# Half-height score products filled up with zeros, and the carried state of two heads in one product, in a two-block transformer layer

## The chip, the core and the metric

The kernel runs on one core of a Trainium2 chip. Its time is the device time of one execution in microseconds (us); several executions give a median. The engines named here are TensorE (matrix products, results in PSUM), VectorE, ScalarE, GpSimd and the DMA queues that SyncE issues.

## The reference, cut to what matters

Two transformer blocks run one after the other on 512 tokens of width 1024. The first block's mixer adds a chunked state-space scan and a causal attention with forget gates. The second block has a sliding-window attention, a gated spatial mixer and 32 routed experts. The parts that the change touches:

```python
# first block, state-space scan: 16 heads of 64, 4 chunks of 128 tokens, state of 128
scores = cb[:, :, None] * decay_in
y_diag = jnp.einsum('bgecls,bcsgep->bclgep', scores, xc)
...
decay_out = jnp.exp(a_cs).transpose(0, 3, 4, 1, 2)
y_off = jnp.einsum('bclgn,bcgepn->bclgep', Cc, prev_states) * decay_out[..., None]
return (y_diag + y_off).reshape(b, s, h, p)

# first block, attention: 16 heads of 64, blocks of 128 queries against all keys up to there
logits = jnp.einsum('bqhd,bkhd->bhqk', q[:, q0:q1], k[:, :q1]) * scale
logits = logits + (cum[:, :, q0:q1, None] - cum[:, :, None, :q1])

# second block, attention: 8 query heads of 64, 2 key heads, window of 128, blocks of 128
scores = jnp.einsum('bnqgrd,bnkgd->bngrqk', q, kb).astype(jnp.float32) * (HEAD_DIM ** -0.5)
```

Here `y_off` is the part of the scan's output that is carried in from earlier chunks, and `y_diag` the part from within a chunk. The 16 heads fall into two groups of eight, which share `Bc` and `Cc`.

## The kernel before, in words

Activations lie transposed: 128 channels in the partitions, 512 tokens in the columns. A tile of 128 channels therefore holds a pair of heads, the even one in partitions 0 to 63 and the odd one in 64 to 127. Weight products are made of three F32R products each (`mm3`, lines 117 to 119): high part by high part, high by low and low by high, where `split_w` makes the parts (ScalarE line 112, VectorE line 113). Products of plain float32 operands show in the profile as two instructions each, F32R ones as one. PSUM has eight banks, which go round among all results (`bank`).

The order of work is made by generators. `proj` runs the eight k-steps of a weight product, three instructions to a step, and after each step `pump` takes the next piece, up to the next `yield`, from a list `side`. A planner of the tile framework then fixes the order on each engine when the program is built, so pieces can move somewhat against each other. The stages that matter here, in order:

- The forgetting attention. `qkv(j)` projects values, queries and keys of pair j with `proj`, and between its steps run `fox_s` (scores and softmax) of pair j-1 and `fox_v` (probabilities by values) of pair j-2. In `fox_s` a head's scores of a block are two products into one PSUM tile. Line 429 is over 128 partitions: the query's high and low parts, one in each half, against the key's high part in both halves. Line 430 is over 64 partitions, the query's high part against the key's low part `kL`, which holds one head in each half. `qkv` fills `kL` at line 516.
- The state-space stage. `ssm_prep` makes the chunk states `st`, then `ssm_pair(j)` runs for eight pairs, between the steps of `zproj` and of the attention half of the output projection (line 667). For each head VectorE and ScalarE make the decay matrix `dec` (lines 607 to 610; one buffer for each of the two heads) and scale a copy of C by the head's decay (`csb`, lines 612 and 613). Then TensorE adds up, for each head and chunk, the product with `dec` (line 621) and, from the second chunk on, the product of the head's 64 state columns with `csb` (line 623). Each fills 64 of the 128 output partitions. After the eight pairs the scan's output is split into `ysH` and `ysL` (lines 683 and 684) and projected.
- The second block's attention. `att_s` (line 890) has products over the 64 partitions in which the head's queries lie. The key tile `kd` holds one key head in both halves, so that it can meet a query head in either. `att_v` follows two items later, and `gate_j` (line 971) runs in between, with products into the lower and the upper 64 output partitions by turns.

Feed-forward and experts follow in their places and are not touched.

Of the kernel before, what the change touches and what calls it, by code (L numbers as in the profile page):

```python
# [10 lines left out]
F32 = mybir.dt.float32  # L11
# [10 lines left out]
P = 128  # L22
T = 512
# [27 lines left out]
def tile_kernel(ctx, tc, I, out, dbg=None):  # L51
# [359 lines left out]
    ya = [keep.tile([P, T], F32, name=f"ya{j}", tag=f"ya{j}") for j in range(8)]  # L411
    fox = {}

    def fox_s(j, b):

        qA, kA, kL, vt = fox[j]
        h = 2 * j + b
        r = slice(b * 64, (b + 1) * 64)
        cumb = pf.tile([P, T], F32, name="cumb", tag="cumb", bufs=2)
        sp.dma_start(cumb[:, None, :], rowd[16 + h:17 + h, :].partition_broadcast(P))  # L420
        cumd = pf.tile([P, 4, P], F32, name="cumd", tag="cumd", bufs=2)
        pool.affine_select(cumd, cumb.rearrange("p (c n) -> p c n", c=4), pattern=[[0, 4], [-1, P]],
                           compare_op=OP.is_ge, fill=-NEG, base=0, channel_multiplier=1)
        prs = fox[j, b] = []
        for qb in range(4):
            nk = (qb + 1) * P
            ps = bank("psc")
            qs = slice(qb * P, (qb + 1) * P)
            pe.matmul(ps[:, :nk], qA[b][:, qs], kA[b][:, :nk], start=True, stop=False)
            pe.matmul(ps[:, :nk], qA[b][r, qs], kL[r, :nk], start=False, stop=True)  # L430
            pr = pf.tile([P, nk], F32, name=f"pr{qb}", tag=f"pr{qb}", bufs=3)
            mx = pf.tile([P, 4], F32, name="mx", tag="mx", bufs=8)
            if qb:
                dve.tensor_tensor_reduce(out=pr[:, :qb * P], in0=ps[:, :qb * P], in1=cumb[:, :qb * P], scale=1.0,
                                         scalar=NEG, op0=OP.subtract, op1=OP.max, accum_out=mx[:, 0:1])
            dve.tensor_tensor_reduce(out=pr[:, qb * P:], in0=ps[:, qb * P:nk], in1=cumd[:, qb], scale=1.0,
                                     scalar=mx[:, 0:1] if qb else NEG, op0=OP.subtract, op1=OP.max,
                                     accum_out=mx[:, 1:2])
            dve.tensor_scalar(mx[:, 2:3], mx[:, 1:2], -1.0, None, op0=OP.mult)
            act.activation(pr, pr, AF.Exp, bias=mx[:, 2:3], accum_out=mx[:, 3:4])  # L440
            dve.reciprocal(mx[:, 3:4], mx[:, 3:4])
            dve.tensor_scalar(pr, pr, mx[:, 3:4], None, op0=OP.mult)
            prs.append(pr)
            yield

    def fox_v(j, b):

        qA, kA, kL, vt = fox[j]
        prs = fox[j, b]
        yp = bank("yap")  # L450
        r = slice(b * 64, (b + 1) * 64)
        pts = {}

        def tr(kb):
            n = T - kb * P
            ps = bank("ppt")
            for qb in range(kb, 4):
                pe.transpose(ps[:, (qb - kb) * P:(qb - kb + 1) * P], prs[qb][:, kb * P:(kb + 1) * P], ident)
            ph_ = pf.tile([P, n], F32R, name=f"pH{kb}", tag=f"pH{kb}", bufs=1)
            pl_ = pf.tile([P, n], F32R, name=f"pL{kb}", tag=f"pL{kb}", bufs=1)  # L460
            act.copy(ph_, ps[:, :n])
            dve.tensor_sub(pl_, ps[:, :n], ph_.bitcast(F32))
            pts[kb] = (ph_, pl_)

        def pv(kb):
            pe.matmul(yp[:, kb * P:], vt[:, kb, b, :], pts[kb][0], start=kb == 0, stop=False, skip_group_check=True)
            pe.matmul(yp[:64, kb * P:], vt[:, kb, b, :64], pts[kb][1], start=False, stop=kb == 3,
                      skip_group_check=True)

        tr(0)  # L470
        yield
        for kb in range(1, 4):
            tr(kb)
            yield
            pv(kb - 1)
            yield
        pv(3)
        t = pf.tile([64, T], F32, name="yt", tag="yt", bufs=2)
        act.copy(t, yp[64:])
        dve.tensor_add(ya[j][r], yp[:64], t)  # L480
        yield
        if b == 1:
            add_sq(pf, sqa, ya[j], j)

    def qkv(j, rate):
        pv_ = bank("pv")
        proj(I["w_v"][j], pv_, hH, hL, rate)
        ada(None, 32 + j)
        vf = pf.tile([P, T], F32, name="vf", tag="vf", bufs=1)
        act.copy(vf, pv_)  # L490
        pq = bank("pq")
        proj(I["w_q"][j], pq, hH, hL, rate)
        ada(None, 16 + j)
        qA = [pf.tile([P, T], F32R, name=f"qA{b}", tag=f"qA{b}", bufs=2) for b in range(2)]
        kA = [pf.tile([P, T], F32R, name=f"kA{b}", tag=f"kA{b}", bufs=2) for b in range(2)]
        kL = pf.tile([P, T], F32R, name="kL", tag="kL", bufs=2)
        vt = pf.tile([P, 4, 2, P], F32R, name="vt", tag="vt", bufs=3)
        rr = [slice(0, 64), slice(64, 128)]
        for b in range(2):
            r, o = rr[b], rr[1 - b]  # L500
            act.mul(qA[b][r], pq[r], 0.125)
            dve.scalar_tensor_tensor(qA[b][o], pq[r], 0.125, qA[b][r].bitcast(F32), op0=OP.mult, op1=OP.subtract)
        pvt = bank("pvt")
        for c in range(4):
            pe.transpose(pvt[:, c * P:(c + 1) * P], vf[:, c * P:(c + 1) * P], ident)
        p4 = pvt.rearrange("p (c b d) -> p c b d", c=4, b=2)
        act.copy(vt[:, :, :, :64], p4)
        dve.tensor_sub(vt[:, :, :, 64:], p4, vt[:, :, :, :64].bitcast(F32))
        pk = bank("pk")
        proj(I["w_k"][j], pk, hH, hL, rate)  # L510
        ada(None, 24 + j)
        for b in range(2):
            r, o = rr[b], rr[1 - b]
            act.copy(kA[b][r], pk[r])
            act.copy(kA[b][o], pk[r])
            dve.tensor_sub(kL[r], pk[r], kA[b][r].bitcast(F32))
        fox[j] = (qA, kA, kL, vt)

    for j in range(8):
# [78 lines left out]
    def ssm_pair(j):  # L598
        g = j // 4
        work = []  # L600
        for b in range(2):
            h = 2 * j + b
            csb = px.tile([P, T], F32, name="csb", tag="csb", bufs=4)
            sp.dma_start(csb[:, None, :], rowd[h:h + 1, :].partition_broadcast(P))
            dec = px.tile([P, 4, P], F32, name="dec", tag=f"dec{b}", bufs=1)
            for c in range(4):
                dve.scalar_tensor_tensor(dec[:, c], csb[:, c * P:(c + 1) * P], cs3[:, c, h:h + 1], cmask,
                                         op0=OP.subtract, op1=OP.add)
            act.activation(dec, dec, AF.Exp)
            dve.tensor_mul(dec, dec, cbt[g])  # L610
            yield
            act.activation(csb[:, P:], csb[:, P:], AF.Exp)
            dve.tensor_mul(csb[:, P:], csb[:, P:], bc[2 + g][:, P:])
            work.append((dec, csb))
            yield
        yp = bank("yp")
        for b, (dec, csb) in enumerate(work):
            h = 2 * j + b
            for c in range(4):
                o = yp[b * 64:(b + 1) * 64, c * P:(c + 1) * P]  # L620
                pe.matmul(o, xc[c][:, h * 64:(h + 1) * 64], dec[:, c], start=True, stop=c == 0)
                if c:
                    pe.matmul(o, st[c - 1][:, h * 64:(h + 1) * 64], csb[:, c * P:(c + 1) * P],
                              start=False, stop=True)
                if c % 2:
                    yield
        dve.scalar_tensor_tensor(ys[j], ys[j], col("d_skip", j), yp, op0=OP.mult, op1=OP.add)
        dve.tensor_mul(ys[j], ys[j], zs[j])
        add_sq(px, sqs, ys[j], j)
        dump("ys", ys[j], j)  # L630
        yield
# [212 lines left out]
        for f in range(6):  # L844
            mm3(pb8[f], wh[:, f], wl[:, f], x2H[k], x2L[k], k == 0, k == 7)

    kd = [sb.tile([P, T], F32, name=f"kd{i}") for i in range(2)]
    sg_ = [sb.tile([P, T], F32, name=f"sg{k}") for k in range(4)]
    vt2 = sb.tile([P, 4, P], F32, name="vt2")
    gel = [sb.tile([P, T], F32, name="gf", tag="gf", bufs=4) for _ in range(4)]  # L850
# [11 lines left out]
    for kv in range(2):  # L862
        r = slice(kv * 64, kv * 64 + 64)
        for hf in range(2):
            act.activation(kd[kv][hf * 64:(hf + 1) * 64], pb8[0][r], AF.Identity, bias=cols[r, o2 + 4:o2 + 5])
    vf = pin.tile([P, T], F32, name="vf2", tag="pr2", bufs=3)
    act.activation(vf, pb8[1], AF.Identity, bias=col("b_in2", 5))
    for j in range(2):
# [10 lines left out]

    def att_s(j, b, n0, box):  # L880
        kv, h = j // 2, 2 * j + b
        r = slice(b * 64, b * 64 + 64)
        ps = bank("ps2")
        pr = pin.tile([P, 2, 2 * P], F32, name="pr2", tag="pr2", bufs=3)
        prf, o0 = pr.rearrange("p a n -> p (a n)"), P if n0 == 0 else 0
        for i in range(2):
            n = n0 + i
            k0 = max(n - 1, 0) * P
            q0 = i * 2 * P + (P if n == 0 else 0)
            pe.matmul(ps[:, q0:(i + 1) * 2 * P], qt2[j][r, n * P:(n + 1) * P], kd[kv][r, k0:(n + 1) * P],  # L890
                      start=True, stop=True)
        s_ = pin.tile([P, 8], F32, name="st2", tag="st2", bufs=4)
        if o0:
# [980 lines left out]
```

## Time and profile before

| | before |
|---|---|
| median of 3 runs (lowest to highest) | 2283.87 us (2282.76 to 2285.36) |
| profiled execution: its time, and its span | 2284.27 us, 2282.4 us |
| TensorE busy, mean granted clock | 94% of the span, 0.974 |
| VectorE busy | 64% |
| ScalarE busy | 48% |
| GpSimd busy | 8% |
| DMA | 243 GB/s mean; 0.44 of the time in the first attention, about 1.0 in the experts |

Busy time of TensorE is counted from modelled ends, and its products overlap, so a share near 100% tells only that it hardly ever waits. How fast it works is seen in the distance from one start to the next. The granted clock is a share of 2.4 GHz.

### The profile page before, as it was taken

The page shows a single profiled execution, that of the slowest core. Times are in us where ns is not written, and L with a number is a line of the kernel's source. Part 1 is how long each engine was busy: PE and PEld are TensorE (multiplying, and loading weights), DVE is VectorE, ACT ScalarE, POOL GpSimd, SP SyncE. Part 2 cuts the span into 40 slices and gives each one's busy share as a digit, 9 for nine tenths or more (in the row PEclk, how much of TensorE's full clock was granted, in tenths as well). Part 3 has the DMA queues.
Part 4 walks back from the last instruction along what each step waited for, and adds up shares of the span by engine and source line. Part 5 has one row for each costly group of instructions (what it writes and reads, how often), then busy time and mean ns, then how long its engine had stood idle before and what let it go on. Part 6 is the DMA issues. An engine that isn't in the chain of part 4 may idle for free. (4 is left out here: it accounts for less than half of the span.)

```text
span 2282.4 us, 27704 instructions
## 1 busy us (share of the span) xinstructions
PE 2156.6 (94%) x9794; PEld 1502.9 (66%) x9795; DVE 1450.0 (64%) x2620; ACT 1102.7 (48%) x1511; POOL 188.5 (8%) x159
## 2 busy tenths in 40 slices
PE   7999999999999998999799999999999999899995
PEld 5777777677887886768677665456555765445653
DVE  7999977776324547563799665547544565645565
ACT  2576674434434444672477454335542455244453
POOL 0001100210000001001301110000000101001001
PEclk9999999999999998999799999999999999999998
DMA  8454323333422333216799999999996999999892
GB/s 281 138 152 143 118 70 118 102 94 122 130 98 91 90 101 89 74 65 232 262 336 369 368 391 397 404 395 360 395 383 248 372 396 397 392 364 380 343 378 81
DMA packets 153488, 554.54 MB, mean 243 GB/s; under 512 B 13440, under 2 KB 13824, under 8 KB 153344
## 3 DMA queue, kind: packets, MB, share of 16 engines
q1 hardware_dynamic: 143888, 527.54, 62.4%
q0 software_dynamic: 9456, 25.18, 4.5%
q8 instruction: 79, 1.29, 0.2%
q14 instruction: 65, 0.53, 0.1%
HBM read 537.91 MB, written 19.99 MB: 244 GB/s over the span
## 5 line engine op out<-in xcount | busy, mean ns | idle before, releaser
L1302 DVE TENSOR_TENSOR el<-eraw,eh 128x1024 fp32r<-128x1024 f32 x428 | 502.0, 1219 | 91.8 <-ACT eh L1301 80.6
L1301 ACT CAST eh<-eraw 128x1024 fp32r<-128x1024 f32 x432 | 439.4, 1049 | 136.0 <-PE ps_G L1368 48.5
L113 DVE TENSOR_TENSOR wl<-wraw,wh 128x1024 fp32r<-128x1024 f32 (+1 forms) x150 | 181.6, 1211 | 215.0 <-ACT wh L112 214.5
L112 ACT CAST wh<-wraw 128x1024 fp32r<-128x1024 f32 (+1 forms) x150 | 153.9, 1026 | 283.6 <-PE pff L118 88.9
L1369 PE MATMUL ps_G<-el,BH 128*128 128x512 f32 x288 | 114.7, 398 | 1.7 <-DVE el L1302 1.5
L1367 PE MATMUL ps_D<-eh,AH 128*128 128x512 f32 x272 | 110.4, 406 | 6.0 <-ACT eh L1301 6.0
L1367 PE MATMUL ps_G<-eh,BH 128*128 128x512 f32 x288 | 115.2, 400 | 0.0
L1369 PE MATMUL ps_D<-el,AH 128*128 128x512 f32 x272 | 111.2, 409 | 3.8 <-DVE el L1302 3.7
L1368 PE MATMUL ps_G<-eh,BL 128*128 128x512 f32 x288 | 113.3, 393 | 0.0
L1368 PE MATMUL ps_D<-eh,AL 128*128 128x512 f32 x272 | 108.4, 399 | 0.0
L1383 PE MATMUL ps_D<-eraw,AW 128*64 128x512 f32 x448 | 106.5, 603 | 0.0
L1383 PE MATMUL ps_G<-eraw,BW 128*64 128x512 f32 x448 | 103.8, 597 | 0.0
L117 PE MATMUL pff<-h2H,wh 128*128 128x512 f32 x256 | 101.1, 399 | 2.0 <-ACT h2H L721 2.0
L1369 PE MATMUL ps_U<-el,BH 128*128 128x512 f32 x256 | 101.9, 398 | 0.3 <-DVE el L1302 0.3
L119 PE MATMUL pff<-h2H,wl 128*128 128x512 f32 x256 | 101.4, 396 | 0.2 <-DVE wl L113 0.2
L117 PE MATMUL pfo<-fh,wh 128*128 128x512 f32 x256 | 99.4, 391 | 1.9 <-ACT fh L745 1.9
L1383 PE MATMUL ps_U<-eraw,BW 128*64 128x512 f32 x448 | 101.2, 604 | 0.0
L118 PE MATMUL pfo<-fl,wh 128*128 128x512 f32 x256 | 100.9, 395 | 0.0
L1367 PE MATMUL ps_U<-eh,BH 128*128 128x512 f32 x256 | 100.6, 393 | 0.0
L1368 PE MATMUL ps_U<-eh,BL 128*128 128x512 f32 x256 | 100.6, 393 | 0.0
L118 PE MATMUL pff<-h2L,wh 128*128 128x512 f32 x256 | 100.5, 393 | 0.0
L119 PE MATMUL pfo<-fh,wl 128*128 128x512 f32 x256 | 99.6, 392 | 0.0
(953 smaller groups left out, 4541.1 us busy)
## 6 DMA issues: line engine op xcount, KB each, us to landing
eraw<-in_w_gate_dram SPq DMA_DIRECT2D x128, 1024.0 KB, 10.5
eraw<-in_w_up_dram SPq DMA_DIRECT2D x127, 1024.0 KB, 10.8
eraw<-in_w_down_dram SPq DMA_DIRECT2D x127, 1024.0 KB, 11.2
wada<-in_w_ada_dram SPq DMA_DIRECT2D x48, 512.0 KB, 4.4
wraw<-in_w_fo_dram SPq DMA_DIRECT2D x32, 512.0 KB, 3.4
wraw<-in_w_ff_in_dram SPq DMA_DIRECT2D x26, 512.0 KB, 3.4
wraw<-in_w_out_dram SPq DMA_DIRECT2D x16, 512.0 KB, 3.9
wraw<-in_w_xs_dram SPq DMA_DIRECT2D x8, 512.0 KB, 6.9
```

What stands on the lines that cost most here:

```text
L112: act.copy(h, w)
L113: dve.tensor_sub(l, w, h.bitcast(F32))
L117: pe.matmul(ps, wh, xh, start=first, stop=False)
L118: pe.matmul(ps, wh, xl, start=False, stop=False)
L119: pe.matmul(ps, wl, xh, start=False, stop=last)
L1301: act.copy(h, raw_k)
L1302: (pool if ns[0] < 4 else dve).tensor_sub(l, raw_k, h.bitcast(F32))
L1367: pe.matmul(ps[:, hf], xh[:, k], h[:, s_], start=k == 0 and bias is None, stop=False)
L1368: pe.matmul(ps[:, hf], xl[:, k], h[:, s_], start=False, stop=False)
L1369: pe.matmul(ps[:, hf], xh[:, k], l[:, s_], start=False, stop=k == 7)
L1383: pe.matmul(ps[hf * 64:(hf + 1) * 64, 0], x[:, k], raw[:, hf * 512:(hf + 1) * 512], start=k == 0 and bias is None, stop=k == 7)
```

## The change

Three places change.

1. The key's low part gets a tile for each head of the pair. The half that belongs to the other head is zeroed once by GpSimd, before the loop, in two sets of tiles that take turns. Line 430's product then runs over 128 partitions; what meets the zeros adds nothing. To make room, `yt` has one buffer in place of two.
2. In `ssm_pair` the carried part isn't added up with the rest. One product for each chunk from the second on takes both heads' 128 state columns against the unscaled C, into a PSUM tile of its own. The decay is put on its result: ScalarE fills one tile `ecs` with both heads' exponentials, 64 partitions each, VectorE multiplies it by the product and adds it to the output. The products with `dec` go chunk by chunk, the two heads in turn.
3. The second block's key tile `kd` becomes two, one for each half, with zeros in the other half, and line 890's product runs over 128 partitions.

```diff
+    kLz = [[pf.tile([P, T], F32R, name=f"kL{i}{b}") for b in range(2)] for i in range(2)]
+    for i in range(2):
+        for b in range(2):
+            pool.memset(kLz[i][b][(1 - b) * 64:(2 - b) * 64].bitcast(F32), 0.0)
...
             pe.matmul(ps[:, :nk], qA[b][:, qs], kA[b][:, :nk], start=True, stop=False)
-            pe.matmul(ps[:, :nk], qA[b][r, qs], kL[r, :nk], start=False, stop=True)
+            pe.matmul(ps[:, :nk], qA[b][:, qs], kL[b][:, :nk], start=False, stop=True)
...
-        t = pf.tile([64, T], F32, name="yt", tag="yt", bufs=2)
+        t = pf.tile([64, T], F32, name="yt", tag="yt", bufs=1)
...
-        kL = pf.tile([P, T], F32R, name="kL", tag="kL", bufs=2)
+        kL = kLz[j % 2]
...
-            dve.tensor_sub(kL[r], pk[r], kA[b][r].bitcast(F32))
+            dve.tensor_sub(kL[b][r], pk[r], kA[b][r].bitcast(F32))
...
-            act.activation(csb[:, P:], csb[:, P:], AF.Exp)
-            dve.tensor_mul(csb[:, P:], csb[:, P:], bc[2 + g][:, P:])
-            work.append((dec, csb))
+
+            r = slice(b * 64, (b + 1) * 64)
+            if b == 0:
+                ecs = csb
+            act.activation(ecs[r, P:], csb[r, P:], AF.Exp)
+            work.append(dec)
             yield
+
+        yo = bank("yo")
+        for c in range(1, 4):
+            tk = slice(c * P, (c + 1) * P)
+            pe.matmul(yo[:, tk], st[c - 1][:, j * P:(j + 1) * P], bc[2 + g][:, tk], start=True, stop=True)
+        yield
         yp = bank("yp")
-        for b, (dec, csb) in enumerate(work):
-            h = 2 * j + b
-            for c in range(4):
-                o = yp[b * 64:(b + 1) * 64, c * P:(c + 1) * P]
-                pe.matmul(o, xc[c][:, h * 64:(h + 1) * 64], dec[:, c], start=True, stop=c == 0)
-                if c:
-                    pe.matmul(o, st[c - 1][:, h * 64:(h + 1) * 64], csb[:, c * P:(c + 1) * P],
-                              start=False, stop=True)
-                if c % 2:
-                    yield
+        for c in range(4):
+            for b, dec in enumerate(work):
+                h = 2 * j + b
+                pe.matmul(yp[b * 64:(b + 1) * 64, c * P:(c + 1) * P], xc[c][:, h * 64:(h + 1) * 64], dec[:, c],
+                          start=True, stop=True)
+            if c % 2:
+                yield
+        dve.tensor_mul(ecs[:, P:], yo[:, P:], ecs[:, P:])
         dve.scalar_tensor_tensor(ys[j], ys[j], col("d_skip", j), yp, op0=OP.mult, op1=OP.add)
+        dve.tensor_add(ys[j][:, P:], ys[j][:, P:], ecs[:, P:])
...
-    kd = [sb.tile([P, T], F32, name=f"kd{i}") for i in range(2)]
+    kd = [[sb.tile([P, T], F32, name=f"kd{i}{b}") for b in range(2)] for i in range(2)]
+    for i in range(2):
+        for b in range(2):
+            pool.memset(kd[i][b][(1 - b) * 64:(2 - b) * 64], 0.0)
...
-            act.activation(kd[kv][hf * 64:(hf + 1) * 64], pb8[0][r], AF.Identity, bias=cols[r, o2 + 4:o2 + 5])
+            act.activation(kd[kv][hf][hf * 64:(hf + 1) * 64], pb8[0][r], AF.Identity, bias=cols[r, o2 + 4:o2 + 5])
...
-            pe.matmul(ps[:, q0:(i + 1) * 2 * P], qt2[j][r, n * P:(n + 1) * P], kd[kv][r, k0:(n + 1) * P],
+            pe.matmul(ps[:, q0:(i + 1) * 2 * P], qt2[j][:, n * P:(n + 1) * P], kd[kv][b][:, k0:(n + 1) * P],
                       start=True, stop=True)
```

## Rows read from the trace of the kernel before

**Rows 1.** Windows: start:end length, busy us (instructions) by engine, TensorE's clock, DMA share.

```profile
130.00:290.00 160.00, 159.72 (x743) 117.58 (x743) 145.27 (x485) 101.15 (x224) 15.57 (x16) 1.00 0.44 135
290.00:318.00 28.00, 27.53 (x129) 19.81 (x129) 23.14 (x86) 19.43 (x42) 1.90 (x2) 1.00 0.23 67
...
370.00:452.00 82.00, 81.74 (x432) 59.54 (x430) 59.23 (x125) 40.61 (x59) 13.08 (x6) 1.00 0.33 114
...
452.00:470.00 18.00, 15.21 (x58) 12.29 (x58) 12.29 (x17) 10.57 (x16) 1.78 (x1) 0.81 0.18 56
...
930.00:1020.00 90.00, 86.21 (x453) 60.68 (x452) 62.77 (x200) 67.54 (x137) 0.00 (x0) 0.99 0.15 48
```

**Rows 2.** Waits of TensorE, 130 to 290 us: total, times, longest.

```profile
PE pq L117 <- ACT wh L112: 0.3, 1, 0.3
```

**Rows 3.** Waits of VectorE, 130 to 290 us.

```profile
DVE pL L462 <- ACT pH L461: 3.6, 11, 0.5
DVE mx L441 <- ACT pr L440: 3.0, 5, 1.1
```

**Rows 4.** Timeline of TensorE around L564: start, us, instruction, rows*columns, shape, count.

```profile
339.58 0.39 PE L119 MATMUL pz<-hH,wl 128*128 128x512 f32 x1
339.81 1.05 PE L564 MATMUL pcb<-bc,bc 128*128 128x128 f32 x8
340.62 0.48 PE L117 MATMUL pz<-hH,wh 128*128 128x512 f32 x1
```

**Rows 5.** Timeline of TensorE around one L430.

```profile
206.23 0.40 PE L429 MATMUL psc<-kA,qA 128*128 128x512 f32 x1
206.56 0.49 PE L430 MATMUL psc<-kL,qA 64*128 64x512 f32 x1
206.98 0.50 PE L117 MATMUL pk<-hH,wh 128*128 128x512 f32 x1
207.31 0.40 PE L118 MATMUL pk<-hL,wh 128*128 128x512 f32 x1
```

**Rows 6.** Timeline of TensorE, one head of a state-space pair.

```profile
371.28 0.39 PE L119 MATMUL pz<-hH,wl 128*128 128x512 f32 x1
371.60 0.65 PE L621 MATMUL yp<-dec,xc 128*64 128x128 f32 x4
...
372.40 0.50 PE L117 MATMUL pz<-hH,wh 128*128 128x512 f32 x1
372.74 0.40 PE L118 MATMUL pz<-hL,wh 128*128 128x512 f32 x1
...
373.30 0.43 PE L621 MATMUL yp<-dec,xc 128*64 128x128 f32 x2
...
374.32 0.49 PE L117 MATMUL pz<-hH,wh 128*128 128x512 f32 x1
```

**Rows 7.** Timeline of TensorE, products into both output halves by turns.

```profile
950.08 0.66 PE L971 MATMUL psg<-wsp,gx 128*64 128x128 f32 x8
950.67 0.50 PE L117 MATMUL pj<-x2H,wh 128*128 128x512 f32 x1
```

**Rows 8.** VectorE by line, 370 to 452 us: busy, mean ns | idle before, releaser.

```profile
L607 DVE SCALAR_TENSOR_TENSOR dec<-csb,cs,cmask 128x128 f32<-128x128 f32 x56 | 18.4, 385 | 6.1 <-PE yp L621 5.8
...
L610 DVE TENSOR_TENSOR dec<-dec,cbt 128x512 f32<-128x512 f32 x15 | 10.2, 682 | 0.0
L613 DVE TENSOR_TENSOR csb<-csb,bc 128x384 f32<-128x384 f32 x15 | 8.2, 550 | 0.0
L627 DVE SCALAR_TENSOR_TENSOR ys<-ys,cols,yp 128x512 f32<-128x512 f32 x8 | 6.0, 746 | 15.4 <-PE yp L623 15.4
```

**Rows 9.** Timeline of TensorE behind the last pair.

```profile
454.21 0.49 PE L117 MATMUL pa__4457<-ysH,wh 128*128 128x512 f32 x1 [2.04 <-ACT ysH L683]
```

**Rows 10.** Timeline of TensorE, one group of the second attention's scores.

```profile
985.57 0.92 PE L890 MATMUL ps<-kd,ya 64*128 64x128 f32 x4
986.42 0.50 PE L117 MATMUL pj<-x2H,wh 128*128 128x512 f32 x1
```

More of the change, by code (lines that the diff above doesn't have):

```diff
@@ L417, in fox_s @@
         h = 2 * j + b
-        r = slice(b * 64, (b + 1) * 64)
         cumb = pf.tile([P, T], F32, name="cumb", tag="cumb", bufs=2)
@@ L881, in att_s @@
         kv, h = j // 2, 2 * j + b
-        r = slice(b * 64, b * 64 + 64)
         ps = bank("ps2")
```

## The prediction

> **What bounds the kernel now.** I read the page's busy shares first (TensorE is busy for most of the span, VectorE for two thirds), then the windows of each stage that the change touches, then the lists of waits there, then the timeline of TensorE alone. The windows [rows 1] show in the forgetting attention (130 to 290 us) TensorE busy for 159.7 of 160 us and VectorE for 145.3; in the state-space stage (370 to 452) TensorE for 81.7 of 82 and VectorE for 59.2; in the second attention (930 to 1020) TensorE for 86.2 of 90. The waits agree: from 130 to 290 us TensorE waited 0.3 us for anyone [rows 2]. So TensorE sets the pace of all three. The reader should see also how near the next engine is: VectorE has only 14.7 us of idle time in those 160, and part of it is not TensorE's doing, since it waits for ScalarE in steps that go VectorE, ScalarE, VectorE [rows 3].
>
> A busy TensorE isn't one at its peak, so the timeline has to be read by starts. At its usual pace a product of 512 columns hands over to the next after 0.23 us (the first two starts of [rows 4]). Around L430, which uses 64 partitions, the starts are 0.33, 0.42 and 0.33 us apart [rows 5]. From L429 to the second product behind L430 it is 1.08 us where three at pace take 0.69: 0.39 us lost for one product of 64 partitions. The products of 64 output partitions in the state-space stage [rows 6] show the same: 0.32 us into a group (0.09 over pace), 0.34 after its first successor (0.11 over), and inside it 0.80 us for six instructions and 1.02 for eight, so 0.11 an instruction and some 0.15 besides. (A float32 product shows as two instructions, a rounded one, F32R, as one.) I read that as a toll for going from products that use the whole array to products that use half of it and back.
>
> **Part 1, forgetting attention.** L430 gets 128 partitions, half of them zeros; its columns, so its passes, stay. There are 16 heads with 4 blocks each, 64 products. Each then loses its toll; I keep 0.03 for the weight loads of the narrow ones and take 0.36 us, 23.0 us in all. Bounds: 0 (if the toll came from something else, such as reading two tiles) and 0.39, so 0 to 25. But VectorE lies right behind. From 130 to 290 us there are six rounds of eight products, 17.3 us of saving, and VectorE can't go below 145.3 plus the waits for ScalarE, 6.6 us in the two lines of [rows 3]: about 152. Some of those waits shrink when TensorE runs ahead, so I take 151, which gives 9 us. The last eight products fall into 290 to 318 us, where VectorE is busy for 23.1 of 28: 2.5 of 2.9 us come through. The first eight I count as 0.5. Sum 12 us, between 4 (if nearly every wait of VectorE stays) and 23.
>
> The row says that the half-array product gained nothing from being small: at 512 columns it holds TensorE 0.42 us until the next start, a full one 0.23 [rows 4, 5]. The Trainium skill, page TensorEngine Tiling (Array Packing), section When to Use Tiling, advises the contrary of this change: with 64 or fewer contracted rows, use half-array tiles, two of which can run together. By that rule filling up with zeros would throw away room, and part 1 would lose the 4.6 us of the fourth rival below where the rows promise 23. The trace does not bear it out: in it no half-array product stands next to one in the other half.
>
> What else moves: four memsets of 64x512 on GpSimd before the stage. It is busy for 15.6 of the 160 us of this stage, with 16 instructions [rows 1], and the memsets stand ahead of all of them, so they cost nothing; exposed they would be about a microsecond each, as those 16 are. The one buffer less for yt lets ScalarE's copy wait for VectorE's add of the head before, several us earlier: nothing. The subtraction that fills kL keeps its 64 partitions.
>
> **Part 2, state-space pairs.** Now a pair has two groups of six instructions and two of eight: 2 x (0.80 + 0.20) + 2 x (1.02 + 0.20) = 4.44 us. Afterwards the carried part is three whole-array products, six instructions. The nearest row is L564, same shape: eight in 0.81 us, and 0.23 us into them, at pace [rows 4], so 0.61, taken as 0.7 with the change back to F32R. The diagonal part is two groups of eight, now alternating between the lower and the upper 64 output partitions. L971 alternates in just that way: eight instructions in 0.59 us [rows 7], where eight in one half took 1.02 [rows 6]. With the toll at either end, 0.79 each. New sum 0.7 + 1.58 = 2.28; saved 2.16 a pair, 17.3 us for eight. Without the overlap of the halves a group stays at 1.22: 3.14, saved 10.4. Steps handed to the main loop fall from nine to eight a pair, which moves work but removes none.
>
> VectorE: two multiplications of 0.55 us (L613) go; one of the same width with a PSUM operand and one addition come, 0.55 each taken [rows 8]: nothing. (Bounds for the one with PSUM: the 0.55, and the 0.75 of L627, which reads PSUM over more columns; 1.6 us over all pairs.) ScalarE's exponentials keep their columns. So 59.2 us of VectorE work would meet 64.7 us of TensorE work, and there is a new order among them. The dec buffers are single, one for each head. Today the first head's is free halfway through the pair and the next one is made while TensorE does the second head (VectorE already waits there, 5.8 us at L607 and 15.4 at L627 [rows 8]). Afterwards both come free with the last group only. Behind it stand 0.55 + 0.75 + 0.55 + 0.68 us for the end of the pair (its last multiplication priced as L610, of the same shape), eight L607 (2.6) and two L610 (1.4), then TensorE's 0.79, a main step of 0.69 (three products at pace) and 0.79: 8.8 us, with handing over some 9.4, against 10.3 now (82 us for eight pairs). If that serves as the pace, 7 us are saved; if the planner hides it, 17. I take 9, between 0 and 17.
>
> **Part 3, its end.** When the last pair is through, TensorE waits 2.0 us for ysH [rows 9], and the mean granted clock of 452 to 470 us is 0.81 [rows 1], where it is 1.00 in the stages ahead: after the idle stretch it is at the lower of its levels, 1.2 GHz, for a while. 0.19 of 18 us are 3.4. If the pairs end some steps before the main loop, both go, 5.4 us; if the pairs end last, none. I take 2.
>
> **Part 4, second attention.** Sixteen groups of L890. In one, two products of 128 and 256 columns take 0.85 us [rows 10]: six units of 0.107 are 0.64, 0.21 more. With the 0.20 at the ends of [rows 6], less 0.08 that I leave for going back from float32, it is 0.33, or 5.3 us. Groups next to products of 64 output partitions save less, and TensorE's idle 3.8 us here [rows 1] show that it waits for others at times: 3.5, between 0 and 5.3. The second pair of kd buffers is zeroed by an idle GpSimd.
>
> **Sum.** 12 + 9 + 2 + 3.5 = 26.5 us off 2284.3 (the profiled execution: span 2282.4 and 1.9 around it), which is 0.4 above the median of 2283.9. What follows starts earlier by as much. Against the median: 2258 us.
>
> **Rivals.**
> *All of TensorE's time comes back*: 23 + 17.3 + 5.4 + 5.3 = 51, 2233 us. For it: TensorE hardly ever waits now. Against: VectorE at 91% in one stage, and in the other too after the saving.
> *VectorE becomes the bound in both*: 4 + 2 + 0 + 3.5 = 9.5, 2275 us. For it: the waits for ScalarE and the single dec buffers. Against: VectorE waits for TensorE 21 us in the state-space stage, and those waits shrink.
> *Half-array products run two at a time*: the 64 products have 320 columns on average, 0.23 x 320/512 = 0.144 us, and half of that each, 4.6 us, is given up instead of 12 saved: 16.6 less, 2274 us. Against: L430's 0.42 us, and that its neighbours use the whole array. This is what the page named in part 1 would have.
> *The change does nothing measurable*: the toll comes with something that stays, 2284 us. Against: L564, a whole-array float32 product, stands between F32R products without it [rows 4].
> *Slower*: the chain through the dec buffers, in each pair, with ScalarE's weight casts and table loads in front of its two exponentials. It decides from 12.8 us a pair on (2.5 above today's 10.3, eight times, is 20 us: the 15.5 of parts 1 and 4 and the 0.2% that counts). At 13.3 the stage loses 24 where parts 1 and 4 give 15.5: 2292 us. Against: my count is 9.4.
>
> **How the numbers follow.** Forecast 0.62 (by itself 2247 to 2268), all back 0.12, VectorE in both 0.15, tiles 0.02, nothing 0.04, slower 0.05. The range 2236 to 2275 takes in the forecast, most of what lies towards 2233 and half of what lies around 2275. A difference of 0.2%, 4.6 us, is about what can be told from none. Faster 0.91, same 0.04, slower 0.05.
>
> **What would show it.** Right: L430 and L890 with 128 rows and starts at pace around them; six yo instructions without a toll; groups of eight diagonal instructions in 0.59; TensorE now waiting for wl or pL in the attention, with VectorE above 95%; the first ysH product earlier by some 20 us. Wrong: starts near L430 still 0.3 to 0.4 apart; yp groups at 1.02; L607 waiting for yp longer than today's 5.8 us, with main products done before the pairs; or a gain in one stage given back in a wait for transfers later.

## The result, and the profile after

The changed kernel takes 2259.31 us (median of 5, 2257.69 to 2263.88), the kernel before in the same runs 2285.36 (2282.76 to 2285.62): a ratio of 0.9893 [0.9883, 0.9903], 26.05 us less. 2258 was predicted, from a sum of 26.5. The profiled execution has a span of 2256.5 us, 25.9 less than before, at a mean granted clock of 0.973 (0.974 before).

Where it came from is read off the starts of the first instruction of each stage in TensorE's timeline:

| first start of | before, us | after, us | difference so far |
|---|---|---|---|
| scores (`psc`) | 113.49 | 112.17 | -1.3 |
| state-space stage (`pbt`, L558, now L562) | 333.85 | 317.44 | -16.4 |
| scan's output projection (`pa`) | 454.21 | 430.13 | -24.1 |
| feed-forward (`pff`) | 517.43 | 492.39 | -25.0 |
| second attention (`pj`) | 925.87 | 903.16 | -22.7 |
| its output projection (`po`) | 1024.50 | 997.16 | -27.3 |
| end of the span | 2282.42 | 2256.54 | -25.9 |

So the attention with forget gates became 15.1 us shorter (220.36 to 205.26, first `psc` to first `pbt`), the state-space stage 7.7 (120.36 to 112.69), the second attention 4.6 (98.63 to 94.00). The change doesn't touch the stages in which 1.3 us were gained ahead of the scores, and 2.3 lost around the feed-forward and 1.5 behind `po`. The fourteen kept traces differ by as much there: the first scores start between 110.5 and 115.0 us, and from the first `pff` to the first `pj` it is 407.9 to 411.9 us, in no order that follows the edits.

The windows of the kernel after that answer to [rows 1]: start:end, length, busy us (instructions) of TensorE, its weight loads, VectorE, ScalarE and GpSimd, then TensorE's clock, the DMA share and GB/s.

```profile
128.00:276.00 148.00, 144.46 (x741) 115.64 (x740) 142.78 (x483) 100.63 (x223) 16.78 (x15) 1.00 0.47 145
353.00:428.00 75.00, 67.88 (x385) 50.98 (x383) 61.51 (x126) 41.95 (x60) 9.00 (x6) 1.00 0.38 127
428.00:446.00 18.00, 15.17 (x64) 11.92 (x63) 12.82 (x17) 11.34 (x17) 1.78 (x1) 0.91 0.25 77
903.00:991.00 88.00, 82.48 (x459) 63.78 (x458) 61.63 (x195) 69.45 (x140) 0.00 (x0) 1.00 0.17 54
```

In the first attention 741 instructions of TensorE, where 743 took 160 us, now fit into 148. VectorE is at 96%, and TensorE has 3.5 us idle where it had 0.3. In the state-space stage it has 7.1 of 75 idle. TensorE's longest waits from 60 to 500 us after the change (total, times, longest), against [rows 2], say for what:

```profile
PE yp L633 <- DVE dec L614: 7.1, 6, 2.1
...
PE pa__4441 L117 <- ACT ysH L695: 2.1, 1, 2.1
...
PE yap L471 <- DVE pL L466: 1.8, 5, 0.5
PE yap L470 <- ACT pH L465: 1.7, 4, 0.7
```

TensorE's timeline after, around one product of the scores (L429 and L430 are now L433 and L434), which answers to [rows 5]:

```profile
118.28 0.39 PE L433 MATMUL psc<-kA,qA 128*128 128x512 f32 x1
118.51 0.39 PE L434 MATMUL psc<-kL,qA 128*128 128x512 f32 x1
118.74 0.40 PE L117 MATMUL pq<-hH,wh 128*128 128x512 f32 x1
118.98 0.39 PE L118 MATMUL pq<-hL,wh 128*128 128x512 f32 x1
```

The starts are 0.23, 0.23 and 0.24 us apart: 0.70 where it was 1.08. In a state-space pair (against [rows 6]):

```profile
351.60 0.40 PE L119 MATMUL pz<-hH,wl 128*128 128x512 f32 x1
351.83 0.83 PE L627 MATMUL yo<-bc,st 128*128 128x128 f32 x6
352.42 0.48 PE L117 MATMUL pz<-hH,wh 128*128 128x512 f32 x1
352.74 0.39 PE L118 MATMUL pz<-hL,wh 128*128 128x512 f32 x1
...
355.01 0.39 PE L119 MATMUL pz<-hH,wl 128*128 128x512 f32 x1
355.33 0.66 PE L633 MATMUL yp<-dec,xc 128*64 128x128 f32 x8
355.92 0.50 PE L117 MATMUL pz<-hH,wh 128*128 128x512 f32 x1
```

The six of the carried part take 0.59 us, and 0.09 over pace comes behind them (352.42 to 352.74): 0.68, where 0.7 was taken. The eight diagonal ones take 0.59, as [rows 7] promised, where eight in one half took 1.02. (Only the first pair has a group of eight; in the other seven the planner put two instructions ahead and fourteen together, which take 0.33 to 0.36 us and 1.02.) Both groups were priced rightly; the 7.1 us of waiting for `dec` are the other side. VectorE's lines from 353 to 428 us (busy, mean ns | idle before, releaser) answer to [rows 8]; L611, L614 and L638 were L607, L610 and L627:

```profile
L611 DVE SCALAR_TENSOR_TENSOR dec<-csb,cs,cmask 128x128 f32<-128x128 f32 x56 | 18.9, 381 | 3.4 <-PE yp L633 3.4
L614 DVE TENSOR_TENSOR dec<-dec,cbt 128x512 f32<-128x512 f32 x15 | 12.1, 822 | 2.3 <-ACT dec L613 2.3
...
L638 DVE SCALAR_TENSOR_TENSOR ys<-ys,cols,yp 128x512 f32<-128x512 f32 x8 | 6.0, 745 | 3.0 <-PE yp L633 2.9
...
L639 DVE TENSOR_TENSOR ys<-ys,csb 128x384 f32<-128x384 f32 x8 | 4.4, 552 | 0.0
L637 DVE TENSOR_TENSOR csb<-yo,csb 128x384 f32<-128x384 f32 x8 | 4.4, 548 | 0.0
```

The two new instructions cost 0.55 us each, the one that reads PSUM too. VectorE's waits for `yp`, 21.2 us before, are 6.3, and TensorE, which before waited for no `dec`, now waits 7.1 us for it.

In the second attention (L890 is now L905) four instructions take 0.47 us where [rows 10] have 0.85, and the product behind them 0.42 where [rows 6] have 0.34:

```profile
959.84 0.82 PE L905 MATMUL ps<-kd,ya 128*128 128x128 f32 x4
960.31 0.58 PE L117 MATMUL pj<-x2H,wh 128*128 128x512 f32 x1
960.73 0.39 PE L118 MATMUL pj<-x2L,wh 128*128 128x512 f32 x1
```

### The profile page after: what moved, and what is told of

Read it like the earlier page. It is cut to its first block, busy times and chain, and to the rows that moved or that the text cites. A ratio compares the mean times of both kernels' runs of the same rounds, so it can differ in the third digit from the quotient of the medians.

```text
span 2256.5 us, 27626 instructions
## 1 busy us (share of the span) xinstructions
PE 2118.9 (94%) x9746; PEld 1495.8 (66%) x9747; DVE 1448.4 (64%) x2620; ACT 1104.4 (49%) x1511; POOL 190.4 (8%) x167
## 5 line engine op out<-in xcount | busy, mean ns | idle before, releaser
L1383 PE MATMUL ps_G<-eh,BL 128*128 128x512 f32 x288 | 113.3, 393 | 0.0
L1383 PE MATMUL ps_D<-eh,AL 128*128 128x512 f32 x272 | 108.9, 400 | 0.0
L1383 PE MATMUL ps_U<-eh,BL 128*128 128x512 f32 x256 | 100.4, 392 | 0.0
```

The costliest lines, as they stand in the source:

```text
L1383: pe.matmul(ps[:, hf], xl[:, k], h[:, s_], start=False, stop=False)
```

## The experiments

### Each part alone, and the half rows put back

The theory: part 1's time is the toll of products over 64 rows among products over 128, part 2's gain is held by the single `dec` buffers, and the parts add up. The rivals: the time came from something else that came along (buffers, another order), or one part does it all. Three kernels are the kernel before with one part of the change each. The fourth is the changed kernel, zeros and tiles and all, with only the rows of one product cut back:

```diff
+        r = slice(b * 64, (b + 1) * 64)
-            pe.matmul(ps[:, :nk], qA[b][:, qs], kL[b][:, :nk], start=False, stop=True)
+            pe.matmul(ps[:, :nk], qA[b][r, qs], kL[b][r, :nk], start=False, stop=True)
```

> The kernel before with the first part alone (zero-filled low key part in the forgetting attention, one yt buffer). Toll theory: the attention stage ends about 16 us earlier, as it does in the changed kernel, and nothing else moves by more than 2 us: 2269 us, between 2266 and 2272. Rival, the parts help each other through a new plan of the order: less than 10 or more than 22 us from this part alone.

> The kernel before with the second part alone (carried state as one product for two heads, diagonal products with the heads in turn). Toll theory, with the single dec buffers as the new limit: 7 to 8 us less from the state-space stage, 2277 us, between 2274 and 2280, and TensorE waits some 7 us for VectorE's dec. Rival, VectorE's added work or the later release of csb eats the gain: no gain here alone, 2283 to 2286.

> The kernel before with the third part alone (zero-filled key tiles in the second block's attention). Toll theory: 4.6 us less as in the changed kernel, 2280 us, between 2278 and 2282. Rival, that stage waits for ScalarE and VectorE, and what it gained in the changed kernel came from its new order: under 2 us.

> The changed kernel with all its tiles and zeros, but the low score product reads only the 64 partitions that hold the head, as before. Toll theory: the distances of the starts around that product go back to 0.33, 0.42 and 0.33 us and the attention stage to about its old length: 2275 us, between 2272 and 2278. Rival, the separate key tiles or the new plan brought the gain, not the rows of the product: stays near 2260.

All four came out inside the ranges expected of the toll.

| kernel | us | ratio to before (2285.01) | less |
|---|---|---|---|
| scores alone | 2270.27 | 0.9935 [0.9918, 0.9951] | 14.7 |
| pairs alone | 2278.35 | 0.9968 [0.9957, 0.998] | 6.7 |
| second attention alone | 2279.62 | 0.9976 [0.9967, 0.9986] | 5.4 |
| all, with half rows in the scores | 2275.94 | 0.9963 [0.9949, 0.9977] | 9.1 |

The three add up to 26.8; the whole change gave 26.05. With the half rows back the stretch from the first `psc` to the first `pbt` is 220.39 us, where it was 220.36 before and 205.26 with full rows (205.37 with the scores alone). Nothing else differs between the two, so the rows of this one product are the cause. TensorE's timeline of the kernel with half rows (L433 to L434 are L434 and L435 there) has the old distances of 0.33, 0.42 and 0.34 us:

```profile
120.88 0.40 PE L434 MATMUL psc<-kA,qA 128*128 128x512 f32 x1
121.21 0.49 PE L435 MATMUL psc<-kL,qA 64*128 64x512 f32 x1
121.63 0.50 PE L117 MATMUL pq<-hH,wh 128*128 128x512 f32 x1
121.97 0.40 PE L118 MATMUL pq<-hL,wh 128*128 128x512 f32 x1
```

The Trainium skill, page TensorEngine Tiling (Array Packing), section Key Properties, states that changing from one tiling to another drains TensorE. These four rows agree in that the change costs time, 0.39 us for one product and the way back; that TensorE drains they don't show.

### What holds the pairs

If the buffers hold them, a second one for each head takes the waits for `dec` away, and the rest of the 17.3 us comes through. The rival: the order of the eight diagonal products, head by head as before, would free the first head's buffer early and so be as good, without the overlap of the halves. Both start from the changed kernel.

```diff
-            dec = px.tile([P, 4, P], F32, name="dec", tag=f"dec{b}", bufs=1)
+            dec = px.tile([P, 4, P], F32, name="dec", tag=f"dec{b}", bufs=2)
```

(`btok`, which shares the tag, gets `bufs=2` too.) And, by head:

```diff
-        for c in range(4):
-            for b, dec in enumerate(work):
+        for b, dec in enumerate(work):
+            for c in range(4):
...
-            if c % 2:
-                yield
+            yield
```

> The changed kernel, but the diagonal products of a pair go one head after the other again. Overlap theory: eight instructions in one output half take 1.02 us instead of 0.59, so TensorE has 0.43 us more to do in 16 groups, 7 us; against that the first head's dec buffer comes free early again, and TensorE's 7 us of waiting for dec shrink. Together 2256 to 2264 us, with groups of eight at 1.02. Rival, the two halves never overlapped and the gain came from the shared carried product alone: groups of eight unchanged near 0.59.

> The changed kernel with two dec buffers for each head instead of one. Chain theory: TensorE's 7.1 us of waiting for dec in the state-space stage go down to 2 or less, VectorE starts the next pair's decay while TensorE is at this one, and the time falls by 4 to 8 us, to 2251 to 2255. Rival, VectorE's amount of work sets the pace of that stage (61.5 us busy of 75): the waits move elsewhere, 2258 to 2260.

By head: 2259.17 us, 0.9887 [0.987, 0.9903], the same as the changed kernel. Two buffers: 2248.64, 0.9838 [0.9822, 0.9854], 10.7 less than the changed kernel and below the 2251 to 2255 expected. TensorE's timeline by head, one group:

```profile
361.25 1.09 PE L633 MATMUL yp<-dec,xc 128*64 128x128 f32 x8
362.27 0.50 PE L117 MATMUL pb__3852<-yaH,wh 128*128 128x512 f32 x1
```

Eight take 1.02 us again, twice in each of eight pairs: 16.3 us, where the groups of the changed kernel take 11.1, so 5.2 more (6.9 was expected). But TensorE's waits of that kernel from 330 to 470 us have only one for `dec`, 3.0 us where the changed kernel waits 7.1:

```profile
PE yp L633 <- DVE dec L614: 3.0, 1, 3.0
```

That one wait costs more than itself: from 403 to 413 us, around it, the mean granted clock is 0.66, and 1.00 in the 10 us before and the 10 us behind, so I estimate 3.4 us more (0.34 of 10). From the first `pbt` to the first `pa` the kernel by head takes 116.88 us, 4.2 more than the changed one. The total is the same even so: the output projection behind is 2.7 us shorter (59.60 us to the feed-forward, with a clock of 1.00 in its first 18 us, against 62.26 and 0.91), and in the profiled execution the scores started 1.7 earlier. So by turns is ahead in the stage itself, and the total doesn't tell the two orders apart.

With two buffers the waits for `dec` are gone with the overlap kept. Whether the order by head would do as well with two buffers was not run. The only wait of that kernel in this stretch, and its window of 67 us:

```profile
PE pa__4441 L117 <- ACT ysH L695: 1.5, 1, 1.5
```

```profile
353.00:420.00 67.00, 67.00 (x386) 50.06 (x385) 58.70 (x125) 44.55 (x63) 9.35 (x6) 1.00 0.40 128
```

TensorE is busy all through, and from the first `pbt` to the first `pa` it takes 104.99 us (changed kernel 112.69, before 120.36): 15.4 of the 17.3 that the starts had promised. The stage gives 7.7 of the 10.7 us; the rest lies in stretches that the edit doesn't touch.

### Whether VectorE's work bounds the attention

The prediction held 11 of part 1's 23 us back because VectorE would be full. Then work taken off VectorE must shorten the stage. First the scaling of the probabilities (L446, 64 instructions, 29.6 us on VectorE) went to ScalarE, in the changed kernel and in the one with two buffers:

```diff
-            dve.tensor_scalar(pr, pr, mx[:, 3:4], None, op0=OP.mult)
+            act.mul(pr, pr, mx[:, 3:4])
```

> The changed kernel, but the scaling of the probabilities by the reciprocal of their sum runs on ScalarE instead of VectorE. VectorE theory: it takes about 24 us of work off VectorE in the 148 us of the attention, TensorE's waits for pL there go, and the stage gives back up to the 5 to 7 us that were missing from 23: 2253 us, between 2250 and 2257. Rival, TensorE still sets the pace, or ScalarE becomes the limit at 126 of 148 us: no gain, 2258 to 2264.

> Two dec buffers and the scaling on ScalarE together. If both theories hold their gains add: 2247 us, between 2243 and 2252. If the time lost is one and the same wait handed on from stage to stage: no better than the better of the two.

2272.9 us, 0.9943 [0.9926, 0.996], and 2262.6, 0.9898 [0.9881, 0.9916]: 13.6 and 14.0 slower. I had expected the contrary. The attention takes 216.86 us in the first, where it took 205.26. The window and ScalarE's longest wait from 128 to 276 us, with the scaling on ScalarE in the changed kernel:

```profile
128.00:276.00 148.00, 137.92 (x688) 109.86 (x687) 120.89 (x403) 116.68 (x254) 14.74 (x15) 0.99 0.44 137
```

```profile
ACT pr L444 <- DVE mx L443: 18.5, 18, 2.4
```

VectorE is busy for 120.9 us, not 142.8, ScalarE for 116.7, and neither is full; ScalarE's exponentials wait 18.5 us for VectorE's maxima (12.9 in the changed kernel), and TensorE gets 688 instructions through instead of 741. This can still be a cost of the new place. So the scaling was left out altogether (that part of the computation is missing), and, with two buffers, was put on GpSimd.

> The changed kernel without the scaling of the forgetting attention's probabilities, so that part of the computation is left out; no other engine takes it over. VectorE theory: about 24 us less work for VectorE in the attention's 148 us and no longer chain anywhere, so TensorE's waits for pH and pL (3.5 us) go and the stage runs at TensorE's pace: 2251 to 2255 us. Rival, TensorE sets the pace of the stage already, and what was missing from 23 us was never there: 2257 to 2261.

> Two dec buffers, and the scaling of the probabilities on GpSimd, which is nearly idle. If VectorE's amount of work limits the attention and the scaled probabilities are not needed soon: 2242 to 2246 us against the 2248.6 with the two buffers alone. Rival, GpSimd slows VectorE down when both run, or its part of the chain is late: 2249 to 2260.

Without the scaling the experts get other tokens and more work (9,954 instructions of TensorE in all against 9,746), so the total of 2358.7 us, 1.0331 [1.0314, 1.0348], says nothing here; the stage does. It takes 206.85 us, not less than 205.26. Its window and TensorE's waits from 128 to 276 us:

```profile
128.00:276.00 148.00, 143.13 (x730) 114.79 (x729) 129.41 (x429) 99.22 (x219) 14.58 (x15) 1.00 0.46 146
```

```profile
PE yap L470 <- DVE pL L465: 2.6, 5, 0.8
PE yap L469 <- ACT pH L464: 2.0, 5, 0.7
```

VectorE has 18.6 us to spare, and TensorE still waits for `pL` and `pH`, 4.6 us where it waited 3.0 in the same window of the changed kernel. So less work on VectorE alone doesn't shorten this stage. With the scaling on GpSimd and two buffers the time is 2253.85 us, 0.9871 [0.985, 0.9893], 5 more than on VectorE; VectorE is busy for 128.4 us of the same window, and the attention takes 208.29.

### The end of the pairs, and a longer way to the values

Behind the last pair the changed kernel waits as long as before [rows 9]. The timeline of several engines there:

```profile
427.65 0.40 PE L119 MATMUL pb__4361<-yaH,wl 128*128 128x512 f32 x1
427.89 1.04 ACT L112 CAST wh<-wraw 128x1024 fp32r<-128x1024 f32 x1 [6.08 <-issue]
...
428.84 0.62 ACT L299 ACTIVATE sqt<-ys 128x512 f32<-128x512 f32 x1
...
429.37 1.32 ACT L695 ACTIVATE ysH<-ys,cols 128x512 fp32r<-128x512 f32 x2
...
430.13 0.50 PE L117 MATMUL pa__4441<-ysH,wh 128*128 128x512 f32 x1 [2.09 <-ACT ysH L695]
```

ScalarE had been idle for 6.08 us before it started a cast of weights just after TensorE's last product of the old weights had begun, and `ysH` stands behind that cast. I read this as the cast waiting for the weight buffer to come free; the profile names nothing that it waited for. In the kernel with two `dec` buffers that one cast was then held behind the `ysH` splits, in the order in which they are written:

```diff
-        act.copy(h, w)
+        i_ = act.copy(h, w)
+        if pin:
+            tc.keep_in_program_order(i_)
...
-            proj(I["w_out"][ob, :, :8], ps, ysH, ysL, 0, rms, (4, 7) if ob == 0 else ())
+            proj(I["w_out"][ob, :, :8], ps, ysH, ysL, 0, rms, (4, 7) if ob == 0 else (), pin=ob == 1)
```

The last kernel adds to it one more step between the transposes of probabilities and the product that uses them (`fox_v`), against the waits for `pH` and `pL`.

> Two dec buffers, and ScalarE's cast of the second weight block of the scan's output projection is put behind the eight splits into ysH in ScalarE's order. Queue theory of the stage's end: ysH stood behind a cast that waits until TensorE is done with the block before; with it out of the way TensorE's wait for ysH (1.5 us) falls below 1 us and the time by 1 to 3 us, 2245.5 to 2247.5. Rival, ysH waits for the last pair itself: no change, 2248 to 2250.

> The kernel of two dec buffers and the later cast, and in the forgetting attention the product of the probabilities with the values comes one step later behind its transposes. Distance theory: from the transposes over ScalarE's pH and VectorE's pL takes longer than the shortened TensorE work in between, so one more step takes away TensorE's waits for pH and pL; the stretch from the first score product to the first transposes of the state-space stage goes from 205.4 to 201 to 203 us, and the time to 2243 to 2246. Rival, those waits are VectorE's backlog and come back at the later place: stretch within 1 us of 205.4, time 2247 to 2250.

With the cast held: 2247.65 us, 0.9842 [0.9826, 0.9859]. Against the kernel before in the same runs that is no better than without it (0.9838). But the gap is gone from TensorE's timeline; what is left are waits of 0.6 us for `wl` and 0.4 for `ysL`:

```profile
421.66 0.39 PE L121 MATMUL pb__4361<-yaH,wl 128*128 128x512 f32 x1
421.89 0.40 PE L119 MATMUL pa__4441<-ysH,wh 128*128 128x512 f32 x1
```

With the longer way: 2249.77 us, 0.9855 [0.9838, 0.9873]. The attention took 208.76 us, where the kernel without this step took 205.39, and TensorE's waits from 128 to 276 us grew from 3.0 to 6.1:

```profile
PE yap L472 <- ACT pH L467: 4.8, 5, 1.6
PE yap L473 <- DVE pL L468: 1.3, 4, 0.6
```

One more step in between did not take the waits away. The two kernels with two `dec` buffers, with the cast held and without, are the fastest that were measured, 11.7 and 10.7 us below the changed one, and can't be told apart.

## Why the prediction was right, and where its steps were off

The time was right, and so was its first reason, the toll read from [rows 5]: shown both ways, by the scores alone and by the half rows put back. The size and the second reason of part 1 were not, and that the total is nearly met is in part luck.

**Part 1: 12 predicted, 15.1 measured.** The 23 us of toll do not all come through, but VectorE's floor of 151 us was the wrong working for the rest: 741 of the 743 instructions ran in 148 us, of which VectorE was busy for 142.8, and with 13.4 us less of VectorE work the stage was no shorter. Worked out from all starts of the stretch, the time over columns at pace (512 in 0.213 us at 2.4 GHz) fell from 53.1 to 38.0 us. The price of the toll held: at the three distances from L429 to the second product behind L430 it fell from 26.4 to 6.1 us in the 59 pairs that stand directly in a row, 0.34 us each where 0.36 was taken. At starts of products of probabilities by values that follow `pk`, `pv` or `pz` it rose from 2.2 to 6.6: part of the toll came back as waits for `pH` and `pL`. What sets those waits stays open. Less work on VectorE and more steps in between both left them; but each of these edits also let the planner order the stage anew, so a chain between the engines (ScalarE's exponentials waited 12.9 us for VectorE's maxima in the changed kernel) is a guess that no run isolates.

**Part 2: 9 predicted, 7.7 measured** (6.7 alone), between 0 and 17. The chain through the single buffers was named, and two buffers show it. The 9.4 us a pair of that count meant 7 us for the stage; I took 2 more for what the planner would hide, and it hid under one. That [rows 6] show the same toll as [rows 5] was read too broadly, as the last section tells.

**Part 3: 2 predicted, 1.0 measured.** The pairs did not end earlier than the main loop: the gap is 2.09 us where it was 2.04 [rows 9]. From the first `pa` to the feed-forward it is 62.26 us, before 63.22. The mean granted clock of the first 18 us is 0.91 there, not 0.81 [rows 1], so a smaller part of them ran at 1.2 GHz and not at 2.4; why it came back sooner, no run shows. Holding the cast back removed the gap: the stretch from the first `pbt` to the first `pa` fell by 1.7 us (104.99 to 103.32), but the output projection took 1.1 more (60.87 to 61.99).

**Part 4: 3.5 predicted, 4.6 measured** (5.4 alone), at the upper end of the 0 to 5.3 that the rows gave. Two terms of that working were off and largely cancelled: four instructions over full rows take 0.47 us, not the 0.64 taken, and the way back costs 0.19, not 0.08.

With signs: 15.1 + 7.7 + 1.0 + 4.6 = 28.4, and 1.3 ahead of the first scores, less the 2.3 and 1.5 lost in stages that weren't touched: 25.9 of the span. The forecast of 26.5 came so close because part 1 was low by 3.1 and part 4 by 1.1, parts 2 and 3 were high by 2.3, and what the untouched stages lost was not in it. (26.5 off the median of 2283.87 is 2257.4; the 2258 is rounded from the profiled execution's time.)

**The rivals.** Two half-array products sharing TensorE, the third rival (the prediction's part 1 calls it the fourth), would have cost time here; with half rows the stage takes 15.1 us more, so it doesn't hold among neighbours that use the whole array. But the prediction is wrong that no half-array product of the trace stands next to one in the other half. L971 [rows 7] alternates between the output halves, and in the experts of the kernel before two instructions of L1383, which writes the two output halves by turns, start 0.007 us apart (1746.635 and 1746.642 us) and the next two 0.42 us later. So products in two output halves do run together here. Against VectorE as the bound speaks in the first stage the kernel without the scaling, and in the second the one with two buffers, where TensorE is busy for 67 of 67 us beside 58.7 of VectorE. All of TensorE's time back (2233) wasn't reached by any version; the waits for `pH` and `pL` and the losses named above stand in between. The slower case did not come, but its mechanism, the chain through `dec`, cost 7.7 of the 15.4 us that the stage gave with two buffers.

## What to carry to other kernels

Read the distances between starts around every product of another array shape: a half-filled product alone among full ones can cost more than one filled up with zeros. When an edit interleaves two consumers, ask when each of their buffers comes free; here the new order brought nothing in the total without a second buffer, and the second buffer 7.7 us in the stage. And an engine's busy share near 100% is no proof that its work is the limit: take some of the work away before you build on it. Add up the stages before you trust a total that fits.

## What the runs showed of the hardware that I had not expected

Halved output columns did not cost what halved rows did. L467 of the kernel before has 64 output columns (128*64) in F32R among whole-array products, and its timeline shows no toll, 0.23 us from start to start (0.23 is also the median behind its 16 products of 512 columns):

```profile
227.98 0.39 PE L466 MATMUL yap<-pH,vt 128*128 128x512 f32 x1
228.21 0.39 PE L467 MATMUL yap<-pL,vt 128*64 128x512 f32 x1
228.44 0.40 PE L117 MATMUL pq<-hH,wh 128*128 128x512 f32 x1
```

Here what the Trainium skill states of a change of tiling, quoted above, would lead one to expect a distance like that of L430, and the rows have none. In float32 it is less plain. Ahead of the groups of L621 and L633 (128*64) the start comes 0.09 us late, and ahead of the whole-array L627 it does not (0.32 and 0.23). Behind L627, though, the next start but one comes 0.09 us late, about as behind L621. So what [rows 6] show behind a group comes at least in part with float32, and not with the half.

GpSimd took 1,237 ns on average for the 64 scalings that VectorE did in 467, in the rows of L446 from 60 to 310 us, first of the kernel with the scaling on GpSimd, then of the changed kernel:

```profile
L446 POOL TENSOR_SCALAR pr<-pr,mx 128x384 f32<-128x384 f32 (+2 forms) x64 | 78.8, 1237 | 77.1 <-DVE mx L445 68.8 <-DVE mx L443 7.0 <-PE psc L434 1.2
```

```profile
L446 DVE TENSOR_SCALAR pr<-pr,mx 128x128 f32<-128x128 f32 (+1 forms) x64 | 29.6, 467 | 0.8
```
